# Expert retrieval on one core: v as the stationary operand, both coefficient parts as one moving operand, and 24 tokens instead of 16 handled apart, on the v side too

## The chip, the core and the metric

The kernel runs on one core of a Trainium2 chip. The metric is the device time of one execution in microseconds (us). The core's TensorE (PE) multiplies matrices: it loads a stationary operand of up to 128 columns and streams a moving operand past it. VectorE (DVE), ScalarE (ACT) and GpSimd (POOL) do the rest. SyncE (SP), ACT and POOL issue DMA transfers. Each engine works through its own list of instructions in order and waits where an operand is not ready.

## The reference, cut to what matters

One layer of a decoder for 256 tokens of width 1024: a token mixer, then a feed-forward part made of 16384 experts (128 x 128 product keys), of which each token uses 128 (8 heads x 16). The change is in the second part:

```python
q = (hf @ wq).reshape(T, PEER_HEADS, 2, PEER_QDIM // 2)
s = jnp.einsum('thpd,hpnd->thpn', q, subkeys)
s1, i1 = lax.top_k(s[:, :, 0], 16); s2, i2 = lax.top_k(s[:, :, 1], 16)
top_s, pos = lax.top_k(s1[..., :, None] + s2[..., None, :], 16)     # idx: i1*128 + i2 at pos
w = jax.nn.softmax(top_s, axis=-1)
act = jax.nn.gelu(jnp.einsum('cd,chkd->chk', x_c, u[idx_c]))
coef = w_c * act
out = jnp.einsum('chk,chkd->cd', coef, v[idx_c])                    # u, v: 16384 x 1024
```

The result is added to x, and a last RMSNorm with the gain g_last gives the output.

## The kernel before, in words

Everything but the expert part (the mixer, the projection to the queries, the scores) runs until about 275 us and is not touched. After that the kernel does not gather experts for most tokens. It computes all 128 blocks of 128 experts densely, and multiplies by coefficients that are zero nearly everywhere.

**u stage** (`u_pair`, 64 pairs of blocks). Each block of u (128 experts x 1024) is streamed in by SP as a 512 KB tile `raw`, split by ACT into a rounded part `whi` (L192) and by DVE into the rest `wlo` (L196). `block_t` (L364) then makes 24 matmuls for it: 8 chunks of the width, times three products (whi with the tokens' rounded part `ah`, whi with their rest `al`, wlo with `ah`). The moving operand holds the dense tokens, TD = 240 columns. ACT applies Gelu, and the result stays on the chip in `G`, for all 128 blocks. The tiles `raw`, `whi` and `wlo` have three buffers each, and `slot` loads two to three blocks ahead and splits two ahead.

**The hot part of the u stage** (pairs 32 to 63, 64 slots from about 455 us). Beside the blocks, the coefficients of 8 tokens at a time (30 groups) are scattered: DVE writes one-hot rows (`hot_keys`, `hot_high`), ACT scales (`hot_low`), PE multiplies them (`hot_sum`, 16 matmuls, L1293) into a PSUM tile `pw`, and ACT and DVE multiply it into `G` (`hot_copy`, `hot_use`, L1308). The table `at_slot` says in which slot each of these stands: `hot_sum(k)` in slot 2k+2, `hot_use(k)` in slot 2k+3.

**The 16 tokens left out** (NG = 16, two groups of TG = 8). Their 128 experts each are gathered: POOL fetches 128 rows of u by an indirect DMA (`rows_in`, L1083), and DVE multiplies them with the tokens' rows and sums (`dot`, L1089). Their coefficients then go through DMAs and a transpose back into one-hot form (`few_keys`, `few_sum`, 24 matmuls each, L1326, `few_use`) and into `G`, so that for v they are dense columns like the others (256 in all). For the room, the residual `x2` is written out to DRAM and read back.

**v stage** (128 blocks from 662 us). ACT rounds a row of G to `ch` (L1377), DVE takes the rest `cl` (L1378). The stationary operand is 128 tokens of ch or cl, the moving one half of a row block of v (512 columns of whi or wlo): 12 matmuls of 512 columns for each block (`v_part`, L1389), into four PSUM tiles `acc` of 128 tokens x 512. The residual was put there first by 16 transposes (L1411). ch and cl have two buffers each: those of block k+1 are made when block k-1 is done. The last two blocks are done PSUM tile by PSUM tile, so that the closing norm of a tile can begin while PE works on the next.

## Time and profile before

| what | value |
|---|---|
| median of 3 runs | 1021.89 us (1021.51 to 1022.21) |
| the profiled execution's own time | 1019.87 us |
| its span, first to last instruction | 1018.1 us |
| PE busy | 1003.4 us (99%) |
| DVE busy | 761.1 us (75%) |
| ACT busy | 597.3 us (59%) |
| moved by DMA | 192.87 MB, 189 GB/s over the span |

The span is shorter than the execution's own time by 1.8 us, which lie ahead of the first instruction and behind the last. PE's busy time counts matmuls whose ends are modelled, so 99% says that PE nearly always had a matmul in flight, not that each is as short as it can be. What one matmul costs in a stream is read from start to start: the time of a piece of the chain divided by the number of matmuls in it.

### The profile page before, as it was taken

What the parts mean: (1) busy time and instruction counts of PE and PEld (TensorE: products, weight loads), DVE (VectorE), ACT (ScalarE), POOL (GpSimd) and SP (SyncE); (2) the same over time, 40 slices, a digit from 0 to 9 for tenths busy, and PEclk for the clock granted to TensorE, in tenths of its full rate; (3) what the DMA queues carried; (4) which work ended last, traced back from release to release, by engine and by line L of the source; (5) the groups of instructions that cost most, each with busy time, mean ns of one, the idle gap of its engine ahead of it and who ended that gap; (6) DMA issues with size and microseconds to landing.
All of it is one profiled execution on the core that took longest, in us unless ns stands there. A gap on an engine that the chain in (4) does not pass through costs nothing.

```text
span 1018.1 us, 18964 instructions
## 1 busy us (share of the span) xinstructions
PE 1003.4 (99%) x7394; PEld 926.0 (91%) x7394; DVE 761.1 (75%) x1423; ACT 597.3 (59%) x1090; POOL 53.8 (5%) x69
## 2 busy tenths in 40 slices
PE   9999999999999999999999999999999999999997
PEld 7898999999999999999999999988888888888885
DVE  5888676877889987868999999756666666666664
ACT  7554445665555655648888777545455455454454
POOL 3000010000010001120111100000000000000000
PEclk9999999999999999999999999999999999999999
DMA  8733444566486657675566545545555555555562
GB/s 275 244 103 105 125 113 140 166 199 189 155 286 210 210 192 249 217 279 183 209 209 208 185 153 187 181 166 189 201 189 192 200 186 195 198 189 195 195 211 101
DMA packets 54938, 192.87 MB, mean 189 GB/s; under 512 B 6512, under 2 KB 7968, under 8 KB 54816
## 3 DMA queue, kind: packets, MB, share of 16 engines
q1 hardware_dynamic: 48816, 175.27, 52.2%
q0 software_dynamic: 4448, 14.74, 4.3%
q10 hardware_dynamic: 1584, 1.64, 0.5%
q8 instruction: 58, 0.95, 0.4%
q14 instruction: 32, 0.26, 0.1%
HBM read 188.40 MB, written 3.23 MB: 188 GB/s over the span
## 4 chain that ended last, share of the span: by engine, by line
PE 93%; DVE 4%; ACT 2%; DMA 1%; issue 0%; DVEq 0%; ACTq 0%
PE pj L364 47%; PE acc L1389 34%; PE pw L1293 3%; DVE wlo L196 1%; DMA raw<-in_u_t 1%; PE pS L655 1%; ACT whi L192 1%; PE pT L627 1%; PE pS L496 1%; PE pS L1170 1%; PE pO L286 1%; PE pO L638 0%; PE pO L639 0%; PE pj L760 0%; PE pj L757 0%
## 5 line engine op out<-in xcount | busy, mean ns | idle before, releaser
L196 DVE TENSOR_TENSOR wlo<-raw,whi 128x1024 fp32r<-128x1024 f32 (+2 forms) x329 | 398.9, 1213 | 126.3 <-ACT whi L192 125.3
L192 ACT ACTIVATE whi<-raw 128x1024 fp32r<-128x1024 f32 (+2 forms) x329 | 343.2, 1045 | 125.9 <-PE pj L364 51.2
L364 PE MATMUL pj<-ah,whi 128*128 128x240 f32 (+1 forms) x1344 | 321.3, 282 | 0.3 <-ACT whi L192 0.3
L364 PE MATMUL pj<-al,whi 128*128 128x240 f32 (+1 forms) x1344 | 314.9, 277 | 0.0
L364 PEld LDWEIGHTS pj<-al,whi 128*128 128x128 f32 x1344 | 255.0, 190 | 1.2 <-issue 1.0
L364 PEld LDWEIGHTS pj<-ah,whi 128*128 128x128 f32 x1344 | 254.1, 189 | 2.0 <-issue 1.2
L364 PE MATMUL pj<-ah,wlo 128*128 128x240 f32 (+1 forms) x1344 | 181.1, 277 | 0.0
L364 PEld LDWEIGHTS pj<-ah,wlo 128*128 128x128 f32 x1344 | 166.0, 189 | 0.0
L1389 PE MATMUL acc<-whi,ch 128*128 128x512 f32 x512 | 158.6, 390 | 0.0
L1389 PE MATMUL acc<-wlo,ch 128*128 128x512 f32 x512 | 158.5, 389 | 0.0
L1389 PE MATMUL acc<-whi,cl 128*128 128x512 f32 x512 | 158.5, 390 | 0.0
L1377 ACT ACTIVATE ch<-G 128x256 fp32r<-128x256 f32 x128 | 53.4, 418 | 171.3 <-PE acc L1389 171.3
L1389 PEld LDWEIGHTS acc<-whi,cl 128*128 128x128 f32 x512 | 96.1, 188 | 20.2 <-DVE cl L1378 0.3
L1389 PEld LDWEIGHTS acc<-whi,ch 128*128 128x128 f32 x512 | 96.0, 188 | 20.2 <-ACT ch L1377 0.3
L1389 PEld LDWEIGHTS acc<-wlo,ch 128*128 128x128 f32 x512 | 96.1, 188 | 19.9
L1378 DVE TENSOR_TENSOR cl<-G,ch 128x256 fp32r<-128x256 f32 x128 | 54.4, 426 | 69.5 <-ACT ch L1377 69.5
L1281 ACT ACTIVATE onehot<-onehot,wl 128x128 f16<-128x128 f16 x240 | 76.4, 392 | 18.3 <-DVE onehot L1285 17.6
L364 PE MATMUL pj<-bh,whi 128*128 128x256 f32 x192 | 48.0, 286 | 0.0
L364 PE MATMUL pj<-bl,whi 128*128 128x256 f32 x192 | 47.4, 284 | 0.0
L1293 PE MATMUL pw<-onehot 128*128 128x128 f16 x480 | 33.3, 220 | 4.1 <-DVE G L1308 2.5
L622 ACT ACTIVATE prob<-pS,nm 128x128 f32<-128x128 f32 (+1 forms) x48 | 19.7, 416 | 29.1 <-DVE nm L619 29.1
L1274 DVE TENSOR_TENSOR onehot<-io,keys 128x2048 f16<-128x2048 f16 x30 | 36.6, 1220 | 0.0
(316 smaller groups left out, 902.3 us busy)
## 6 DMA issues: line engine op xcount, KB each, us to landing
raw<-in_u_t SPq DMA_DIRECT2D x128, 512.0 KB, 3.3
raw<-in_v_n SPq DMA_DIRECT2D x128, 512.0 KB, 3.3
raw<-in_w_m SPq DMA_DIRECT2D x16, 512.0 KB, 3.6
raw<-in_w_q SPq DMA_DIRECT2D x16, 512.0 KB, 3.7
raw<-in_w_t SPq DMA_DIRECT2D x15, 512.0 KB, 4.6
raw<-in_w_b SPq DMA_DIRECT2D x8, 512.0 KB, 3.6
raw<-in_w_o SPq DMA_DIRECT2D x8, 512.0 KB, 3.5
sg<-in_w SPq DMA_DIRECT2D x4, 512.0 KB, 6.7
```

The lines of the kernel that those rows point to most:

```text
L192: return [lambda s=slice(u, min(v, n)): nc.scalar.activation(hi[:, s], raws[k][:, s], AF.Copy) for u, v in cuts]
L196: nc.vector.tensor_tensor(lo[:, cs], raws[k][:, cs], hi[:, cs].bitcast(F32), OP.subtract)
L286: nc.tensor.matmul(wb, warm[:, :P], warm, start=True, stop=True)
L364: nc.tensor.matmul(out, (wl if v == 2 else wh)[:, c], (l if v == 1 else h)[:, c], start=(i == 0), stop=(i == len(seq) - 1))
L496: nc.tensor.matmul(hp[:30, :P], flat(wins[j][:, lp // 8, lp % 8]), w1[:, j, lp], start=(lp == 0), stop=(lp == 15))
L622: nc.scalar.activation(p[:, o], src[b], AF.Exp, bias=nm[:, b:b + 1], accum_out=sums[:, b, h:h + 1])
L1274: nc.vector.tensor_tensor(pairs(E[:, 0:2].rearrange("p s t i -> p (s t) i")), numbers(2 * TG), v[:, :, None, :].to_broadcast([P, 2 * TG, 6 ...
L1281: nc.scalar.activation(E[:, 1, t], E[:, 1, t], AF.Copy, scale=wl[:, n:n + 1])
L1293: nc.tensor.matmul(pw[:, t * P:(t + 1) * P], E[:, 0, t], E[:, 2 - s, t], start=(s == 0), stop=(s == 1))
L1377: nc.scalar.activation(ch, g, AF.Copy)
L1378: nc.vector.tensor_tensor(cl, g, ch.bitcast(F32), OP.subtract)
L1389: nc.tensor.matmul(acc[2 * b + d], (cl if q == 1 else ch)[:, tb], (vl if q == 2 else vh)[:, cs], start=False, stop=last and q == 2, skip_g ...
```

## The change

It does four things.

1. NG goes from 16 to 24: three groups of 8 tokens are left out of the dense part, and TD is 232 instead of 240. There are 29 instead of 30 hot groups.
2. The tokens left out stay out on the v side. Their rows of v are gathered as well (24 more indirect DMAs), and DVE adds them up, weighted, in 24 steps `row_sum` in the v stage, one in every third slot. A group of 8 tokens lies on 128 partitions as 16 parts of 8 tokens. Each group's sums go to DRAM (`ys`, 512 KB), come back with 16 parts side by side (`fold_in`, in runs of 64 numbers), and are added up by DVE (`fold`, a reduction over 1024 numbers in each partition). Their norm and output come from `few_add` to `few_out`. The one-hot path of these tokens (`few_keys`, `few_sum`, `few_use`, `dots_end`, `coefs_in`) and the residual's way through DRAM are gone.
3. In the v stage a block of v is stationary, 128 of its columns at a time, and one tile `co` holds ch and cl side by side (2 x 232 columns) as the moving operand: 8 matmuls of 464 columns with whi and 8 of 232 with wlo. The sums lie transposed, 8 PSUM tiles of 128 of the width x 464. The residual is added by DVE at the end (`finish`), and 16 transposes bring the tokens back into rows (`turn_rows`) ahead of the norm.
4. In the hot part `hot_sum(k)` stands in slot 2k+4 instead of 2k+2, and `dot` in every sixth instead of every fourth slot.

```diff
-NG = 16
+NG = 24
+TB = TD // 2
...
     for k in range(ND):
-        at_slot(2 * k + 2, "pre", hot_sum, k)
-        at_slot(2 * k + 3, "first", hot_copy, k)
-        at_slot(2 * k + 3, "pre", hot_use, k)
...
+        at_slot(2 * k + 4, "pre", hot_sum, k)
+        at_slot(2 * k + 5, "first", hot_copy, k)
+        at_slot(2 * k + 5, "pre", hot_use, k)
...
-        for q in (0, 1, 2):
-            for d in ds:
-                cs = slice(d * 512, d * 512 + 512)
-                nc.tensor.matmul(acc[2 * b + d], (cl if q == 1 else ch)[:, tb], (vl if q == 2 else vh)[:, cs],
-                                 start=False, stop=last and q == 2, skip_group_check=True)
+    def v_high(k, w, c):
+        nc.tensor.matmul(acc[c][:, :2 * TD], w[0][:, c * P:(c + 1) * P], coefs[k], start=(k == 0), stop=False,
+                         skip_group_check=True)
+
+    def v_low(k, w, c):
+        nc.tensor.matmul(acc[c][:, small], w[1][:, c * P:(c + 1) * P], coefs[k][:, :TD], start=False,
+                         stop=(k == P - 1), skip_group_check=True)
...
+    def row_sum(n):
+        q, j = divmod(n, TG)
+        t = rows_of_step(NG + n)
+        w = acts[:, q, j:j + 1]
+        if j == 0:
+            sums_of[0] = oh.tile([P, D], F32, name="ysum", bufs=1)
+            nc.vector.tensor_scalar(sums_of[0], t, w, None, OP.mult)
+        else:
+            nc.vector.scalar_tensor_tensor(sums_of[0], t, w, sums_of[0], OP.mult, OP.add)
+        rows_in(NG + n + 2)
+        if j == TG - 1:
+            nc.gpsimd.dma_start(ys[q], sums_of[0])
+
+    def fold_in(q):
+        nc.gpsimd.dma_start(xq[1].rearrange("p (g d) -> p g d", g=16),
+                            ys[q].rearrange("(g t) (c d) -> (t c) g d", t=TG, c=16))
+
+    def fold(q):
+        r = oh.tile([P, 64], F32, name="fold")
+        nc.vector.tensor_reduce(r, xq[1].rearrange("p (g d) -> p d g", g=16), AX.X, OP.add)
+        nc.gpsimd.dma_start(yd[q * TG:(q + 1) * TG].rearrange("t (c d) -> (t c) d", c=16), r)
...
+    for n in range(NG):
+        at_slot(26 + 3 * n, "v", row_sum, n)
+    for q in range(NQ):
+        n = 26 + 3 * (TG * q + TG - 1)
+        at_slot(n + 2, "v", fold_in, q)
+        at_slot(n + 6, "v", fold, q)
...
+    def finish(c):
+        for k in (P - 2, P - 1):
+            v_high(k, ends[k], c)
+            v_low(k, ends[k], c)
+        xc = x2c(c)[:, NG:]
+        nc.vector.tensor_tensor(xc, xc, acc[c][:, small], OP.add)
+        lasts[c] = oh.tile([P, TD], F32, name="last", bufs=3)
+        nc.vector.tensor_tensor(lasts[c], acc[c][:, :TD], xc, OP.add)
```

Where the v stage begins, PE's list read as follows before (pj is the last u block, acc the sums over v):

```order
L364 MATMUL pj<-ah,whi 128x240
L364 MATMUL pj<-al,whi 128x240
L364 MATMUL pj<-ah,wlo 128x240 x8
L1411 MATMUL acc<-ident,x_0_132 128x128 x8
L1411 MATMUL acc<-ident,x_1_133 128x128 x8
L1389 MATMUL acc<-whi,ch 128x512 x2
L1389 MATMUL acc<-whi,cl 128x512 x2
```

and reads now:

```order
L365 MATMUL pj<-ah,whi 128x232
L365 MATMUL pj<-al,whi 128x232
L365 MATMUL pj<-ah,wlo 128x232 x8
L1329 MATMUL acc<-co,whi 128x464 x8
L1333 MATMUL acc<-co,wlo 128x232 x8
```

The transposes between the stages are gone, and the first matmul of a block needs all of co, where it needed ch alone.

In the v stage around slot 53, DVE's list read as follows before (cl and wlo by turns, with buffer numbers):

```order
L1378 TENSOR_TENSOR cl_10169<-G0_2779,ch_10168 128x256
L196 TENSOR_TENSOR wlo_10173<-raw_10144,whi_10172 128x1024
L1378 TENSOR_TENSOR cl_10191<-G0_2779,ch_10190 128x256
L196 TENSOR_TENSOR wlo_10195<-raw_10166,whi_10194 128x1024
L1378 TENSOR_TENSOR cl_10213<-G0_2779,ch_10212 128x256
L196 TENSOR_TENSOR wlo_10217<-raw_10188,whi_10216 128x1024
```

and reads now (ysum is the running row sum, fold the reduction of what fold_in brought into xq):

```order
L1364 TENSOR_SCALAR ysum_10184<-row0_5871,acts_2790 128x1024
L1326 TENSOR_TENSOR co_10205<-G0_2779,co_10205 128x232
L197 TENSOR_TENSOR wlo_10209<-raw_10175,whi_10208 128x1024
L1326 TENSOR_TENSOR co_10230<-G0_2779,co_10230 128x232
L197 TENSOR_TENSOR wlo_10234<-raw_10203,whi_10233 128x1024
L1326 TENSOR_TENSOR co_10255<-G0_2779,co_10255 128x232
L197 TENSOR_TENSOR wlo_10259<-raw_10228,whi_10258 128x1024
L1366 SCALAR_TENSOR_TENSOR ysum_10184<-row1_5872,acts_2790,ysum_10184 128x1024
L1377 TENSOR_REDUCE fold_10264<-xq_5873 128x64
L1326 TENSOR_TENSOR co_10285<-G0_2779,co_10285 128x232
```

A row sum stands behind every third wlo, and in this slot the fold too, ahead of the next block's co.

On POOL the last rows before were these (x is the residual coming back from DRAM):

```order
L1083 DMA x_0_132<-in_u_n,sidx 128x1024 x8
L1097 DMA ads<-x_1_133 128x8
L1112 DMA x_1_133<-ads 8x16x8 x2
L1073 DMA x_0_132<-x2s_2792 128x512 x2
L1073 DMA x_1_133<-x2s_2793 128x512 x2
L1462 TENSOR_SCALAR raw<-raw,lr 128x512
```

and around the first fold they are these now:

```order
L1080 DMA row_5872<-in_v_n,sidx 128x1024
L1369 DMA ys_2798<-ysum 128x1024
L1372 DMA xq<-ys_2798 128x16x64
L1080 DMA row_5871<-in_v_n,sidx 128x1024
L1080 DMA row_5872<-in_v_n,sidx 128x1024
L1378 DMA yd<-fold 128x64
```

POOL, which issued nothing in the v stage, now has the gathers of v there, the way of the row sums through DRAM (ys out, xq back) between them.

## Rows read from the trace of the kernel before

**Rows 1.** The page's busy times and PE's granted clock in 40 slices.
```profile
PE 1003.4 (99%) x7394; PEld 926.0 (91%) x7394; DVE 761.1 (75%) x1423; ACT 597.3 (59%) x1090; POOL 53.8 (5%) x69
PEclk9999999999999999999999999999999999999999
```

**Rows 2.** The page's chain of waits: shares of the span by line.
```profile
PE pj L364 47%; PE acc L1389 34%; PE pw L1293 3%; DVE wlo L196 1%; DMA raw<-in_u_t 1%; PE pS L655 1%; ACT whi L192 1%; PE pT L627 1%; PE pS L496 1%; PE pS L1170 1%; PE pO L286 1%; PE pO L638 0%; PE pO L639 0%; PE pj L760 0%; PE pj L757 0%
```

**Rows 3.** Windows: length, busy of PE, PEld, DVE, ACT, POOL; clock, DMA share, GB/s.
```profile
278.00:455.00 177.00, 176.72 (x1578) 176.53 (x1577) 155.23 (x458) 98.85 (x123) 19.80 (x23) 1.00 0.68 231
463.00:606.00 143.00, 143.00 (x1447) 142.14 (x1447) 133.43 (x185) 119.83 (x297) 13.69 (x10) 1.00 0.57 192
661.92:1005.23 343.31, 343.31 (x1517) 284.29 (x1516) 208.10 (x253) 172.06 (x252) 0.00 (x0) 1.00 0.57 190
```

**Rows 4.** Pieces of the chain in order of time: start, us, what, count.
```profile
219.98 7.68 PE pj L364 x64
...
231.64 0.89 PE pS L1170 x8
...
428.42 21.52 PE pj L364 x192
...
496.43 0.91 PE pw L1293 x16
...
602.15 1.41 PE pw L1326 x24
...
617.98 1.35 PE pw L1326 x24
```

**Rows 5.** PE's timeline at the first hot sum: start, us, what, [idle before].
```profile
455.56 0.23 PE L1293 MATMUL pw<-onehot 128*128 128x128 f16 x1 [0.26 <-DVE onehot L1285]
...
458.10 1.09 PE L1293 MATMUL pw<-onehot 128*128 128x128 f16 x7 [0.96 <-ACT onehot L1281]
```

**Rows 6.** Waits from 463 to 660 us: us, times, longest.
```profile
PE pw L1293 <- DVE G L1308: 2.5, 2, 1.5
```

**Rows 7.** Timeline at the entry to the v stage.
```profile
660.26 1.91 PE L1411 MATMUL acc<-ident,x 128*128 128x128 f32 x16
...
661.64 0.75 DVE L1378 TENSOR_TENSOR cl<-G,ch 128x256 fp32r<-128x256 f32 x2
661.92 0.71 PE L1389 MATMUL acc<-whi,ch 128*128 128x512 f32 x2
```

**Rows 8.** Groups of instructions: busy, mean ns of one, idle before and releasers.
```profile
L196 DVE TENSOR_TENSOR wlo<-raw,whi 128x1024 fp32r<-128x1024 f32 (+2 forms) x329 | 398.9, 1213 | 126.3 <-ACT whi L192 125.3 <-PE pO L354 0.3
L192 ACT ACTIVATE whi<-raw 128x1024 fp32r<-128x1024 f32 (+2 forms) x329 | 343.2, 1045 | 125.9 <-PE pj L364 51.2 <-DMA raw<-in_u_t 34.7 <-issue 10.7
L1378 DVE TENSOR_TENSOR cl<-G,ch 128x256 fp32r<-128x256 f32 x128 | 54.4, 426 | 69.5 <-ACT ch L1377 69.5
L1377 ACT ACTIVATE ch<-G 128x256 fp32r<-128x256 f32 x128 | 53.4, 418 | 171.3 <-PE acc L1389 171.3
L1089 DVE SCALAR_TENSOR_TENSOR x<-x,x 128x1024 f32<-128x1024 f32 x10 | 12.2, 1217 | 0.0
```

**Rows 9.** DMA issues: queue, count, KB each, median us to landing.
```profile
raw<-in_v_n SPq DMA_DIRECT2D x128, 512.0 KB, 3.3
xhs<-xhd POOLq DMA_DIRECT2D x2, 512.0 KB, 6.2
x2s<-x POOLq DMA_DIRECT2D x4, 256.0 KB, 8.8
x<-xhs POOLq DMA_DIRECT2D x2, 512.0 KB, 4.8
...
kcb<-kraw POOLq DMA_DIRECT2D x2, 128.0 KB, 5.4
```

**Rows 10.** Timeline of the kernel's end.
```profile
1010.88 0.60 ACT L1433 ACTIVATE squares<-acc 128x512 f32<-128x512 f32 x1 [0.49 <-PE acc L1389]
...
1012.57 0.88 DVE L1471 SCALAR_TENSOR_TENSOR raw<-acc,lr,x 128x256 f32<-128x256 f32 x2
```

More of the change, by code (lines that the diff above doesn't have):

```diff
@@ L1243, in body @@
             pre = (lambda: tokens_out((e - 4) // 2),), ()
[L1244 to L1246 removed]
+        if e == 16:
             pre = (lambda: tokens_in(0),), ()
[L1248 removed]
+        if 22 <= e < 25:
             pre = (lambda: rows_in(e - 22),), ()
@@ L1258, in body @@
     ps = PB.enter_context(tc.tile_pool(name="pb", bufs=2, space=PSUM, reuse_waits="tile"))
-    G[1] = top.enter_context(tc.tile_pool(name="gb", bufs=1, reuse_waits="tile")).tile([P, 64, T], F32, name="G1")
+    G[1] = top.enter_context(tc.tile_pool(name="gb", bufs=1, reuse_waits="tile")).tile([P, 64, TD], F32, name="G1")
+    wide_rows = top.enter_context(tc.tile_pool(name="rows", bufs=1, reuse_waits="tile"))
+    rows_wide += [wide_rows.tile([P, D], F32, name=f"row{k}") for k in range(2)]
+    xq.append(wide_rows.tile([P, D], F32, name="xq"))
     OH = ExitStack()
@@ L1309, in hot_use @@
         spots["tokens"] += TG
-    few = [flat(t).bitcast(BF).rearrange("p (k t i) -> p k t i", k=2, i=P) for t in x2]
-    def few_keys(q):
-        for s in range(2):
-            nc.vector.tensor_tensor(pairs(few[0][:, s]), numbers(TG),
-                                    keys[:, q, s, :, None, :].to_broadcast([P, TG, 64, 2]), OP.is_equal)
-        for k in range(3):
-            v = cs[:, k, q * TG:(q + 1) * TG, None, :].to_broadcast([P, TG, 64, 2])
-            nc.vector.tensor_tensor(pairs(few[1][:, k] if k < 2 else few[0][:, 1]), pairs(few[0][:, 1]), v, OP.mult)
-    def few_sum(q):
-        pw = wide()
-        for t in range(TG):
-            for k, v in enumerate((few[1][:, 0, t], few[1][:, 1, t], few[0][:, 1, t])):
-                nc.tensor.matmul(pw[:, t * P:(t + 1) * P], few[0][:, 0, t], v, start=(k == 0), stop=(k == 2))
-        hot["few", q] = pw
-    def few_use(q):
-        pv = hot.pop(("few", q)).rearrange("p (t i) -> p i t", t=TG)
-        for k in range(2):
-            nc.scalar.activation(G[k][:, :, q * TG:(q + 1) * TG], pv[:, 64 * k:64 * k + 64], AF.Copy)
     ND = TD // TG
@@ L1406, in v_use, with weights_in, weights_mix @@
-        return f
-    for c in range(NC):
-        for b in range(2):
-            o = acc[2 * b + c // 4][:, (c % 4) * P:(c % 4 + 1) * P]
-            nc.tensor.matmul(o, x2c(c)[:, b * P:(b + 1) * P], ident, start=(c % 4 == 0), stop=False,
-                             is_transpose=True, skip_group_check=True)
+        return f
+    sums_of = [None]
+    def weights_in():
+        nc.scalar.activation(acts, acts, AF.Gelu)
+    def weights_mix():
+        nc.vector.tensor_tensor(acts, acts, mix, OP.mult)
@@ new lines, in few_add, with few_square, few_factor, few_out @@
+    def few_add():
+        nc.vector.tensor_tensor(few[0], few[0], few[1], OP.add)
+    def few_square():
+        nc.scalar.activation(few[1], few[0], AF.Square, scale=1.0 / 32.0, accum_out=fs[:, 0:1])
+    def few_factor():
+        v, r, t, w = (fs[:, k:k + 1] for k in range(1, 5))
+        nc.vector.tensor_scalar(v, fs[:, 0:1], EPS, None, OP.add)
+        nc.scalar.activation(r, v, AF.Sqrt)
+    def few_out():
+        v, r, t, w = (fs[:, k:k + 1] for k in range(1, 5))
+        nc.vector.reciprocal(r, r)
+        nc.vector.tensor_tensor(t, r, r, OP.mult)
+        nc.vector.tensor_tensor(t, t, v, OP.mult)
+        nc.vector.tensor_scalar(t, t, -0.5, 1.5, OP.mult, OP.add)
+        nc.vector.tensor_tensor(w, r, t, OP.mult)
+        nc.vector.scalar_tensor_tensor(few[0], few[0], w, gf[:NG], OP.mult, OP.mult)
+        nc.sync.dma_start(a["out"][0:NG], few[0])
@@ new lines, in body @@
+    for n in range(2 * TG, NG):
+        at_slot(1 + 3 * (n - 2 * TG), "v", dot, n)
+    at_slot(23, "v", weights_in)
+    at_slot(24, "v", weights_mix)
+    for n in range(NG):
+        at_slot(26 + 3 * n, "v", row_sum, n)
+    for q in range(NQ):
+        n = 26 + 3 * (TG * q + TG - 1)
+        at_slot(n + 2, "v", fold_in, q)
+        at_slot(n + 6, "v", fold, q)
+    at_slot(n + 8, "v", few_in)
+    at_slot(n + 12, "v", few_add)
+    at_slot(n + 13, "v", lambda: table(AF.Sqrt))
+    at_slot(n + 13, "v", few_square)
```

239 lines of the change are left out of this document (105 added, 134 removed).

## The prediction

> **What bounds the kernel now.** I read the page's busy times first, then the chain of waits, then windows by stage. PE is busy for 1003.4 of 1018.1 us, at a granted clock of nine tenths or more of the upper level, 2.4 GHz, in all 40 slices [rows 1]. The chain agrees: the block matmuls of the u stage and the projections (L364) hold 47% of the span, those of the v stage (L1389) 34%, and no other engine more than a few per cent [rows 2]. By windows, PE has no idle time in the v stage (343.31 of 343.31 us) nor in most of the hot part, while DVE is busy for 208.10 of 343.31 us in the former and 133.43 of 143.00 us in the latter [rows 3]. So the time is a count of matmuls times the pace of each, plus the few places where PE waits; DVE is the engine that could become the bound.
>
> The pace is read from pieces of the chain in which PE runs without a break [rows 4]: 7.68 us for 64 matmuls of 256 columns is 120.0 ns each, 21.52 us for 192 of 240 columns is 112.1 ns. In the v stage, 343.31 us for 1517 matmuls of 512 columns is 226.3 ns [rows 3]. From 256 to 512 columns a column costs (226.3 - 120.0) / 256 = 0.415 ns. But 8 matmuls of only 128 columns in float32 took 0.89 us, 111.2 ns each [rows 4], against 0.91 us for 16 in 16 bits. So below 240 columns there is a floor for 4-byte operands close to what 240 columns cost.
>
> **The change part by part.** Durations are those of the profiled execution, whose own time is 1019.87 us; the median of the runs shown lies 2.0 us above it, and I carry the difference over to that median.
>
> *Matmuls of the u stage, 240 to 232 columns.* 128 x 24 = 3072 matmuls. If nothing but the floor counts, they stay at 112.1 ns and nothing is saved. If the step from 256 to 240 columns goes on ((120.0 - 112.1) / 16 = 0.49 ns a column), they take 108.2 ns and 12.1 us go. The row nearest in operand type and stationary size is the floor's 111.2 ns, but it has plain float32 operands in short series; I take 110, a little below it: 3072 x 2.1 ns = -6.5 us.
>
> *Matmuls of the v stage.* Before, a block takes 12 x 226.3 = 2716 ns. Now it has 8 of 464 columns, 226.3 - 48 x 0.415 = 206.4 ns each, and 8 of 232 at 110: 2531 ns. That is -0.185 us for each of 126 blocks (the last two are in the tail below), -23.3 us. With 112.1 or 108.2 ns for the small ones it is -21.2 or -25.1. The stationary operands go from 12 to 16 in a block; they cost only through this floor, since in the u stage 24 such loads a block lie beside matmuls half as wide.
>
> The Trainium skill weighs in on this floor: "TensorE: Matmul & The Clock Gate", section "LDWEIGHTS (loading the stationary operand)", gives a load as its columns divided by 1.2 GHz, 106.7 ns for 128, and its section "Back-to-back issue gap" gives a warm matmul as its columns at 2.4 GHz plus 2.5 ns, 102.5 ns for 240. By the greater of the two a u matmul would take 106.7 ns with 240 columns as with 232, so that the u stage would save nothing, and a v block 8 x 195.8 + 8 x 106.7 = 2420 ns instead of 12 x 215.8 = 2590, -21.4 us. The trace's 112.1 and 226.3 ns lie above both figures, so I keep to rows for the size; the direction is a rival below.
>
> *One-hot sums.* One hot group fewer is -0.9 us, the two `few_sum` are 1.41 + 1.35, -2.8 us [rows 4]. Together -3.7.
>
> *Stalls in the hot part.* The first hot sum began at 455.56 and ended at 459.19 us, since ACT and DVE were late with its one-hot rows [rows 5]; it should take 0.9, so with the 0.26 ahead of it 2.9 us were lost. It now stands two slots later, some 5.3 us, which covers that: -2.9. Twice PE waited for DVE to free `pw`, for 2.5 us [rows 6]; both waits stand behind a `few_sum`, which took one of the two buffers, and go: -2.5. What is late next there is DVE: 133.43 of 143.00 us with a dot every fourth slot is 5.94 us in a pair of 6.37; a dot (1.22 us [rows 8]) every sixth slot instead of every fourth takes 0.2 us off a pair, and a pair of PE becomes 48 x 2.1 ns shorter, 6.27. That is 0.92 full on average, more towards the end; I put no stall there. Together -5.4.
>
> *Entry to the v stage.* The 16 transposes took from 660.26 to 661.92 us, and beside them ACT and DVE made the first ch and cl. Gone, they leave PE idle for the same time: the first matmul now needs cl too, which began at 661.64 and takes 0.43 [rows 7, 8], so that it starts at about 662.1. +0.2.
>
> *Row sums and folds.* Let a slot of the v stage be 2.53 us, and T the start of slot 47, in which the first group's last row sum stands. In a slot, ACT makes ch (0.42) and whi (1.05) once PE has left the block before; then DVE has made cl at about 1.1 and wlo at 2.9, and a row sum behind it (1.22, by the dot's row) at 4.15 [rows 8]. The next cl is due at 5.06, so a row sum alone stops nobody, and on average DVE has 2 x 1.65 + 2.85 = 6.15 us of work in three slots, 7.6 us. The fold is another matter. Row sum ends at T + 4.15, `ys` goes out (512 KB), POOL waits for it, then `fold_in` brings 512 KB back in 2048 runs of 256 bytes; the fold stands in slot 53, behind a row sum, and so begins at T + 15.2 + 4.15 at the earliest. Even on time it ends at T + 20.6 (a reduction of 1024 numbers at the row sum's 1.2), and cl behind it is 0.75 us late for PE. In the trace such a write took 6.2 us (`xhs`; 8.8 for the four `x2s`) and a read of the same size 4.8 in 4 KB runs [rows 9]. No row shows one with 2048 runs. From below it takes the 4.8; from above, if runs are what costs, 16 times the 5.4 us that `kcb` took for 128 runs of 1 KB, 86 us. I take twice the nearest row, 10: the way is then 16.2 us, 1.0 over the 15.2 that it has, and the first two folds stop PE for 1.75 each. The third has no row sum ahead of it; by the same count it has 14.4 us and stops PE for 1.8. Together +5.3; from below 1.5.
>
> On such runs the Trainium skill says, in "DMA: Bandwidth & Descriptors", section "Why small descriptors are slow (HBM only)", that 256-byte ones lose 27% to a fixed cost for each. By that `fold_in` would take an estimated 4.8 x 1.27 = 6.1 us and the folds stop PE for 1.5 in all, the end from below; no run here shows it yet.
>
> The gathers of v themselves (24 x 512 KB, one in 7.6 us) add 69 GB/s to 512 KB in 2.53 us, 207. The v stage moved 190 GB/s at a share of 0.57 [rows 3], so 276 would be 0.83. A block's 3.3 us to landing [rows 9] has 5.06 us, two slots, from the freeing of its buffer. I count nothing; if the cover is gone, this is late by what landing exceeds 5.
>
> *Tail.* Before, the last two blocks begin at 1005.23 and the span ends at 1018.1 [rows 3], 12.9 us. Now each of the 8 chunks has 2 x (206.4 + 110) = 633 ns of matmuls, two adds of DVE (0.43 each by cl's row), and two transposes (0.22 by the floor): about 0.85 a chunk on either engine, the last transposes done at 7.9 instead of 5.4. Then ACT has two sums of squares to do (0.60 each [rows 10], and a read-out) where one was left, and the two factors come one after the other. Against the old end, where the last squares began at 1010.88 and the last product at 1012.57 [rows 10], I make that +4.9 in all.
>
> Sum: -6.5 - 23.3 - 3.7 - 5.4 + 0.2 + 5.3 + 4.9 = -28.5, so 991.4 for a profiled execution and 1021.89 - 28.5 = **993.4 us** as a median.
>
> **The rivals.**
>
> *Folds hidden, no floor.* The path through DRAM lands in time (1.5 instead of 5.3), and the small matmuls go on falling to 108.2 ns (u -12.1, v -25.1): 993.4 - 3.8 - 5.6 - 1.8 = 982; with one of the two, 984 to 990. For it: 256 to 240 columns did bring 7.9 ns. Against it: the 111.2 ns of 128 columns.
>
> *The floor holds at 112.1.* Loads of 128 columns already set the pace at 240, so u saves nothing (+6.5) and v 2.1 less: 1002. For it: 111.2 and 112.1 are nearly the same. This is what the skill's rule on loads, weighed above, would make of it.
>
> *DVE becomes the bound.* Late in the hot part `hot_use` covers more blocks and DVE passes PE; at one dot (1.22 us) too much for each of the last four dots that is 4.9: 998. Against it: four slots of lead.
>
> *The folds are late, and the kernel is slower.* DVE stops in order behind each fold, and nothing makes cl meanwhile. The three folds stop PE for 3 x (way - 14.4) or so. All other terms are -33.8, so this decides from 11.3 us a fold: a `fold_in` of over 20 us beside a 6.2 us write. At 26 us it is 3 x 17.8 = 53 and the time 1021.9 - 33.8 + 53 = 1041. For it: 2048 runs have no like in the trace, and the queue shares its engines with v. Against it: 10 us is already twice the nearest row. Between (14 to 20 us) lie 1004 to 1023.
>
> **How the numbers follow.** Forecast 0.52 (its own range 989 to 998), hidden folds or no floor 0.18, floor 0.11, DVE 0.05, folds between 0.08, slower 0.06. The measurement tells 0.2%, 2 us, from no change: the runs before lie within 0.7. Faster 0.93, same 0.01 (out of the late folds), slower 0.06. From 982 to 1006 I leave out most of the late folds and little below, under 2 in 10.
>
> **What would show it.** PE from start to start: near 206 ns for 464 columns, 110 for 232. Windows: about 2.53 us a block in the v stage. The first hot sum at 0.91 us, no wait of `pw` on DVE. In the waits of DVE, the fold on DMA, three times, and PE or its loads on `co` behind it. At the end, some 18 us from the first of the last two blocks. I am wrong if DVE's or ACT's idle time in the v stage vanishes and PE waits there in most slots, or if the block pace is above 2.6 us without such waits.

## The result and the profile after

The changed kernel takes 1012.58 us (median of 4 runs, 1009.96 to 1013.66) against 1021.89 (1021.51 to 1022.21): a ratio of 0.9908, 95% interval 0.9895 to 0.9922. The forecast of 993.4 and its range of 982 to 1006 miss it: 9.3 us were gained where 28.5 were forecast. The profiled run took 1009.96 us. The page's busy times and granted clock, which answer [rows 1]:

```profile
PE 979.0 (97%) x7841; PEld 938.0 (93%) x7841; DVE 791.8 (79%) x1469; ACT 593.0 (59%) x1079; POOL 104.3 (10%) x106
PEclk9999999999999999999999999999999999999996
```

The chain by line, for [rows 2]:

```profile
PE pj L365 50%; PE acc L1329 20%; PE acc L1333 10%; PE pw L1272 3%; PE pS L656 1%; DVE wlo L197 1%; DMA ys<-ysum 1%; PE pT L628 1%; PE pS L497 1%; PE pS L1148 1%; ACT whi L193 1%; DMA xg<-in_x 1%; PE pO L639 0%; PE pO L640 0%; DMA raw<-in_v_n 0%
```

PE is still the bound, but a DMA (`ys<-ysum`) stands in the chain, and in the last slice PE rests and its granted clock falls. Windows put the lost time in its place (start and end, length, busy of PE, PEld, DVE, ACT, POOL, clock, DMA share, GB/s): the u stage from its first narrow matmul to its last, the first 126 blocks of v, and the last two blocks with all that follows. Before:

```profile
275.53:660.42 384.89, 380.55 (x3620) 377.76 (x3618) 340.07 (x716) 263.81 (x525) 35.70 (x37) 1.00 0.61 208
661.92:1004.78 342.86, 342.86 (x1516) 283.91 (x1514) 208.00 (x253) 171.81 (x251) 0.00 (x0) 1.00 0.57 190
1004.78:1018.09 13.31, 6.00 (x25) 4.24 (x23) 4.86 (x17) 6.36 (x15) 1.57 (x1) 0.83 0.21 79
```

and after:

```profile
274.62:647.29 372.67, 372.67 (x3553) 371.70 (x3550) 330.12 (x695) 260.07 (x510) 33.70 (x34) 1.00 0.63 215
649.02:981.72 332.70, 327.09 (x2017) 302.49 (x2017) 242.38 (x304) 172.56 (x257) 53.80 (x41) 1.00 0.74 254
981.72:1008.19 26.47, 7.82 (x50) 6.37 (x48) 10.94 (x32) 5.07 (x13) 0.00 (x0) 0.71 0.11 36
```

| stretch | forecast | measured | missed by |
|---|---|---|---|
| ahead of the u stage | 0 | -0.9 | -0.9 |
| u stage with hot part (-6.5 - 3.7 - 5.4) | -15.6 | -12.2 | +3.4 |
| entry to v | +0.2 | +0.2 | 0 |
| 126 blocks (-23.3 + 5.3) | -18.0 | -10.2 | +7.8 |
| tail | +4.9 | +13.2 | +8.3 |
| sum | -28.5 | -9.9 | +18.6 |

The 0.9 us ahead of the u stage are scatter: in seven other profiles of this document it begins at 274.4 to 276.6 us.

In the u stage an unbroken piece of the chain (start, us, what, count) now reads as below, for [rows 4]: 32.16 us for 288 matmuls is 111.7 ns each, not 110. The first one-hot sum takes 0.91 us, as forecast.

```profile
426.50 32.16 PE pj L365 x288
458.66 0.91 PE pw L1272 x16
```

In the v stage a block without a stop is 8 high matmuls in 1.69 us and 8 low ones in 0.89 (chain from 797 us on): 211 and 111 ns, 2.58 us a block instead of 2.53. So the low ones came as forecast and the high ones are 5 ns dearer.

```profile
797.49 1.69 PE acc L1329 x8
799.18 0.89 PE acc L1333 x8
```

The rest of the 7.8 us is stops. Below are the waits of PE from the second block to the 126th (us, times, longest) and the chain ahead of the longest. With the slower matmuls right behind them the stops cost 7.1 us (332.70 less 126 x 2.584), where 5.3 were forecast.

```profile
PE acc L1329 <- DVE co L1326: 5.6, 4, 2.1
```

```profile
773.31 1.21 DVE ysum L1366
...
774.78 1.98 POOL row L1080
776.75 7.75 DMA ys<-ysum
...
784.60 0.10 DVE ysum L1364
...
785.27 0.41 DVE co L1326
...
785.72 1.96 PE acc L1329 x8
```

The four stops are of 2.13, 0.91, 0.92 and 1.65 us. The first group's last row sum ends at 774.5; POOL issues the next gather ahead of `ys`, `ys` takes 7.75 us, and the second group's first row sum, which overwrites the single `ysum`, holds DVE until it has landed. Behind it stands `co`, for which PE waits. I had looked for waits at the folds' data. They landed in time, in 6.5 us (DMA issues of the v stage, for [rows 9]), and the first two folds, each behind a row sum, stop PE for 0.9 us each by their own length, 1.98 us instead of 1.2; the third, without a row sum ahead of it, stops nobody:

```profile
raw<-in_v_n SPq DMA_DIRECT2D x123, 512.0 KB, 4.2
ys<-ysum POOLq DMA_DIRECT2D x3, 512.0 KB, 6.1
xq<-ys POOLq DMA_DIRECT2D x3, 512.0 KB, 6.5
```

```profile
L1377 DVE TENSOR_REDUCE fold<-xq 128x64 f32<-128x1024 f32 x3 | 5.9, 1981 | 0.0
```

A third kind of stop comes at 955.78, and SP's timeline shows its cause (start, us, queue, line, count): the 24 rows' output, L1408, waited on SP's queue for DVE until 948.36, and the weight loads behind it waited too; the chain then reads `DMA raw<-in_v_n` for 4.22 us, ACT, DVE, PE.

```profile
935.88 5.56 SPq L182 DMA_DIRECT2D raw<-in_v_n  x3
948.36 0.40 SPq L1408 DMA_DIRECT2D out_n<-row  x1
948.85 6.92 SPq L182 DMA_DIRECT2D raw<-in_v_n  x4
```

At the end, the last product (for [rows 10]) starts at 995.44, 13.7 us into the tail where it was 7.8 before: 5.9 more, of the 4.9 forecast, a first wait of 0.6 among them. But from there to the end it is 12.8 us instead of 5.5. The DMA view from 993 to the end, in 40 slices:

```profile
DMA  0000222313122312222222222222222222110000
GB/s 0 0 0 0 65 49 59 65 27 59 59 49 75 59 65 81 81 81 81 75 97 92 75 97 108 102 97 92 102 102 97 102 108 81 75 38 5 0 0 0
```

A share of two to three tenths and some 100 GB/s: the four output transfers of 116 rows keep about a quarter of the engines busy. Before, five transfers of 128 rows (three of 512 columns, two of 256) landed in 2.4 to 3.0 us.

### The profile page after: what moved, and what is told of

Same layout as the page of the kernel before. It is cut to its first block, busy times and chain, and to the rows that moved or that the text cites. A ratio compares the mean times of both kernels' runs of the same rounds, so it can differ in the third digit from the quotient of the medians.

```text
span 1008.2 us, 19956 instructions
## 1 busy us (share of the span) xinstructions
PE 979.0 (97%) x7841; PEld 938.0 (93%) x7841; DVE 791.8 (79%) x1469; ACT 593.0 (59%) x1079; POOL 104.3 (10%) x106
## 4 chain that ended last, share of the span: by engine, by line
PE 91%; DVE 4%; DMA 2%; ACT 1%; issue 1%; POOL 0%; SPq 0%; ACTq 0%; DVEq 0%
PE pj L365 50%; PE acc L1329 20%; PE acc L1333 10%; PE pw L1272 3%; PE pS L656 1%; DVE wlo L197 1%; DMA ys<-ysum 1%; PE pT L628 1%; PE pS L497 1%; PE pS L1148 1%; ACT whi L193 1%; DMA xg<-in_x 1%; PE pO L639 0%; PE pO L640 0%; DMA raw<-in_v_n 0%
## 5 line engine op out<-in xcount | busy, mean ns | idle before, releaser
L365 PE MATMUL pj<-ah,whi 128*128 128x232 f32 (+1 forms) x1344 | 319.2, 280 | 0.0
L365 PE MATMUL pj<-al,whi 128*128 128x232 f32 (+1 forms) x1344 | 313.2, 276 | 0.1
L1329 PE MATMUL acc<-co,whi 128*128 128x464 f32 x1024 | 240.8, 375 | 7.9 <-DVE co L1326 7.9
L1329 PEld LDWEIGHTS acc<-co,whi 128*128 128x128 f32 x1024 | 183.2, 189 | 26.9 <-DVE co L1326 7.4
L365 PE MATMUL pj<-ah,wlo 128*128 128x232 f32 (+1 forms) x1344 | 179.9, 276 | 0.0
L1333 PEld LDWEIGHTS acc<-co,wlo 128*128 128x128 f32 x1024 | 135.0, 190 | 6.3
L1333 PE MATMUL acc<-co,wlo 128*128 128x232 f32 x1024 | 136.9, 274 | 0.0
L1325 ACT ACTIVATE co<-G 128x232 fp32r<-128x232 f32 x128 | 50.7, 397 | 144.3 <-PE acc L1333 144.3
L1326 DVE TENSOR_TENSOR co<-G,co 128x232 fp32r<-128x232 f32 x128 | 50.9, 398 | 33.2 <-ACT co L1325 33.2
L365 PEld LDWEIGHTS pj<-bl,whi 128*128 128x128 f32 x192 | 36.3, 189 | 0.0
```

Source lines behind the costliest of these rows:

```text
L365: nc.tensor.matmul(out, (wl if v == 2 else wh)[:, c], (l if v == 1 else h)[:, c], start=(i == 0), stop=(i == len(seq) - 1))
L1325: nc.scalar.activation(t[:, :TD], g, AF.Copy)
L1326: nc.vector.tensor_tensor(t[:, small], g, t[:, :TD].bitcast(F32), OP.subtract)
L1329: nc.tensor.matmul(acc[c][:, :2 * TD], w[0][:, c * P:(c + 1) * P], coefs[k], start=(k == 0), stop=False, skip_group_check=True)
L1333: nc.tensor.matmul(acc[c][:, small], w[1][:, c * P:(c + 1) * P], coefs[k][:, :TD], start=False, stop=(k == P - 1), skip_group_check=True)
```

## The experiments

Each states its theories' expectations as they stood before it ran; where no other kernel is named, the edit is to the changed one. The diffs are shortened to the lines that carry the edit.

### Output of 116 rows cut into 112 and 4

```diff
-        nc.scalar.dma_start(rows_of(b)[:, halves_of[0]], yo[b][:, halves_of[0]])
+        for r in CUTS:  # slice(0, 112), slice(112, 116)
+            nc.scalar.dma_start(rows_of(b)[r, halves_of[0]], yo[b][r, halves_of[0]])
```

> The changed kernel with each of its four output transfers of 116 rows cut into one of 112 rows and one of 4. Theory (a transfer is shared out over as many DMA engines as divide its rows, and 116 = 4 x 29 leaves 4 of 16): the end, 12 us from the first issue to the last byte before, needs about 4 to 5 us, 7 to 8 us less; median 1004 to 1006 against 1012.6. Rival (the transfers wait behind other traffic or on their queues): no more than 1 us less, and the two more transfers add up to 1 us. Second rival (their lines of 2 KB are slow whatever the rows): no change either.

### Rows at the end as 128 and 104

```diff
-    turned[...][:TB, ...], lasts[c][:, b * TB:(b + 1) * TB]
+    turned[...][:TBS[b], ...], lasts[c][:, CUT[b]]   # 0:128, 128:232; sent as 128, and 96 + 8
```

> The changed kernel with the 232 rows at the end cut into blocks of 128 and 104 rows instead of twice 116, the second sent as 96 and 8 rows. By the theory of the engines (128 and 96 rows over 16, 8 rows over 8) the same gain as the cut in 112 and 4 within 1 us, 1004 to 1006: the small transfer is off the last place's way. By the rivals (other traffic, queue, line length) no change, 1011 to 1014.

The first took 1008.96 us (1003.09 to 1012.01; ratio to the kernel before 0.9854, 0.9817 to 0.9892), the second 1007.12 (1002.83 to 1011.31; 0.9869, 0.9836 to 0.9903). The medians fell by 3.6 and 5.5 us, less than the 7 to 8 forecast, and the runs scatter by 9 us, so the tail itself decides. Second kernel, tail in the windows and DMA view from 994 to the end:

```profile
982.69:1001.06 18.37, 7.83 (x50) 6.37 (x48) 10.93 (x32) 5.07 (x13) 0.00 (x0) 0.81 0.15 52
```

```profile
DMA  0000000002999999900002999999751000000000
```

The tail is 18.37 us instead of 26.47, 8.1 less (in the first kernel, from 991.05 us on, 19.19, 7.3 less), and the engines run at nine tenths, where they ran at two to three. That is the theory; the rivals of queue and line length fall, since queues and lines of 2 KB are the same. The Trainium skill has the rule, in "DMA: Bandwidth & Descriptors", section "Why a DMA increments its semaphore by 16 and not by 1": a transfer goes to the largest number of engines up to 16 that divides its slowest dimension, which for 116 is 4. The share of two to three tenths agrees. Had I weighed it, the 116 rows would have been a rival with some 8 us.

In the first kernel's profile PE waits 10.8 us in the v stage behind its entry, and behind two of its stops, of 3.29 and 2.20 us, the granted clock fell. Windows of the stop and of the block behind it:

```profile
846.00:853.46 7.46, 4.17 (x29) 3.71 (x27) 2.34 (x4) 3.03 (x5) 0.93 (x1) 1.00 0.77 279
853.46:857.58 4.12, 4.12 (x16) 3.77 (x16) 2.52 (x3) 0.15 (x1) 1.64 (x2) 0.59 0.58 198
```

At 0.59 of 2.4 GHz, that is mostly at the lower level of 1.2, the block of 16 matmuls takes 4.12 us for 2.58. So a stop costs more than its length, now and then. This goes some way to explain the scatter: the second kernel's four runs, of 1002.83, 1005.36, 1008.87 and 1011.31 us, had mean granted clocks of 0.995, 0.994, 0.993 and 0.990. The first kernel's do not fall into such an order.

### The waits of the v stage

On top of 128 and 104 rows:

```diff
-            sums_of[0] = oh.tile([P, D], F32, name="ysum", bufs=1)
+            sums_of[0] = oh.tile([P, D], F32, name="ysum", bufs=2)
-        rows_in(NG + n + 2)
         if j == TG - 1:
             nc.gpsimd.dma_start(ys[q], sums_of[0])
+        rows_in(NG + n + 2)
-        at_slot(n + 6, "v", fold, q)
+        at_slot(n + 7, "v", fold, q, 0)   # half the columns each
+        at_slot(n + 8, "v", fold, q, 1)
-        nc.sync.dma_start(a["out"][0:NG], few[0])
+        nc.gpsimd.dma_start(a["out"][0:NG], few[0])
```

> The kernel with 128 and 104 rows at the end, and four edits against the waits of its v stage: two buffers for the row sums, their DMA issued ahead of the next gather, each fold made in two halves two slots apart and one to two slots later, and the 24 rows' output sent on GpSimd's queue instead of SP's. Theory (TensorE's stops at 785, 794, 857 and 955 us of the changed kernel come of these four, and the spread of its runs too, since a stop can cost the clock behind it): the idle time there goes from 0.8 to 2.3 us each to under 0.2, about 5 us less than with the rows alone (1007.1), 1000 to 1003, and a spread under 3 us. Rival (the stops come of late weight loads in a DMA that is 0.75 to 0.84 busy, whatever waits where): they show up elsewhere, 1005 to 1009 with the same spread of 8 to 9 us.

It took 998.90 us (997.81 to 1000.79), ratio 0.978, 0.9762 to 0.9797: 8.2 us less than with the rows alone, and a spread of 3.0 instead of 8.5. The waits of PE in the v stage, and its windows (126 blocks, tail):

```profile
PE acc L1329 <- DVE co L1326: 0.6, 1, 0.6
```

```profile
650.95:978.36 327.41, 326.65 (x2016) 302.21 (x2017) 242.18 (x307) 173.10 (x257) 59.32 (x42) 1.00 0.73 258
978.36:996.80 18.44, 7.82 (x50) 6.36 (x48) 10.94 (x32) 5.07 (x13) 0.00 (x0) 0.84 0.15 52
```

The stops at 785 and 955 us are gone, the second fold's too; 0.6 us stays at the first. There the rival is right: ahead of that stop the chain has `DMA raw<-in_v_n` for 6.90 us, a weight load at the time when the fold's data come in. The four edits were made at once, so which of them took which stop is argued from the chains, not shown by runs of their own; the chains of the stops near 785 and 955 us have the same causes in the profiles of the two kernels above. The profiles with and without the waits differ by 6.1 us in the 126 blocks (333.47 and 327.41), the medians by 8.2.

### The new one-hot table on the kernel before

```diff
-        at_slot(2 * k + 2, "pre", hot_sum, k)
+        at_slot(2 * k + 4, "pre", hot_sum, k)   # its operands in slots 2k to 2k+2
```

> The kernel before with the new table of the one-hot work alone (each sum two slots later, its operands made one to two slots earlier before it). The prediction's step: the first one-hot sum no longer waits for its operands, 2.9 us less, and the two waits for the wide PSUM tile (2.5 us) go only if they come of the table and not of the sums for the 16 tokens. Expected 1019 (2.9 gone) or 1016.5 (both gone). Rival (the wait is taken over by another one in the hot part): 1021 to 1022, no change.

1018.22 us (1017.41 to 1019.97, 9 runs), ratio 0.9968, 0.9954 to 0.9982: 3.1 us, where the interval runs from 1.8 to 4.7. In its profile the first sum still waits for 0.4 us, and the u stage is 2.5 us shorter (382.37 for 384.89). The wait for `pw` is still there (waits of PE, 463 to 660 us), so it belongs to the sums for the 16 tokens, as I had it:

```profile
PE pw L1293 <- DVE G L1308: 2.4, 2, 1.4
```

### Matmuls by width

```diff
+                hi = lambda c: nc.tensor.matmul(acc[c][:, :m], w[0][:, c * P:(c + 1) * P], flat_ah[:, at:at + m], ...)
+                lo = lambda c: nc.tensor.matmul(acc[c][:, to:to + n], w[1][:, c * P:(c + 1) * P], flat_ah[:, at:at + n], ...)
```

> Measures matmuls by width: in the v stage six blocks each with (hi, lo) columns from 512 + 256 down to 400 + 200 on constant moving data in order of all hi then all lo, three of them with a shifted source, a shifted target or hi and lo in turn; in the first half of the u stage 232, 240, 248 and 256 columns by groups of four pairs. It leaves out what the coefficients carry into the sums, so its time is no time of the kernel. The prediction's line through 256 and 512 columns (120.0 and 226.7 ns) gives 206.7 at 464, 213 at 480, 200 at 448, 180 at 400. Theory (464 columns are dear whatever is in them): about 212 at 464 here too, and the widths around tell whether it is a step or a bend. Rival 1 (the data, written by ScalarE and VectorE just before): 206 to 207 here. Rival 2 (the order, eight high ones and then eight low ones): 207 only where hi and lo take turns. Rival 3 (where the data or sums lie, 464 x 4 bytes after a buffer's start): only the shifted groups show 212. For the u stage: floor theory 112 at 232 and 240, 116 to 120 above; no floor 109 to 110 at 232.

Windows over four pairs of u blocks each, 192 matmuls and a few others, at 232, 240, 248 and 256 columns:

```profile
364.60:386.37 21.77, 21.77 (x198) 1.00 0.63 206
386.37:408.02 21.65, 21.65 (x194) 1.00 0.73 258
408.02:430.35 22.33, 22.33 (x197) 1.00 0.60 201
430.35:453.15 22.80, 22.80 (x195) 1.00 0.80 276
```

From 256 to 240 columns 6 ns go, from 240 to 232 none: the floor. Six v blocks of 464 + 232 columns and of 512 + 512:

```profile
766.40:781.92 15.52, 15.52 (x99) 1.00 0.74 271
950.06:972.45 22.39, 22.39 (x98) 1.00 0.58 205
```

2.587 us a block with constant moving data too, so rival 1 falls; rival 3 falls as well (groups with a shifted source or target took 2.59 too). In turn it is 2.561: rival 2 holds in part. The surprise is 512 columns: 233 ns, not the 226.7 of the kernel before.

### Orders, targets, roles

```diff
+                still = lambda c: ah[:, c, 0:P]
+                mm(c % banks, part(h, c), move(0, x))      # 8, 4, 2, 1 targets
+                mm(c, still(c), half(h, c % 2, x))         # weights move
+                mm(2 * b + d, still(q), half(q // 2, d, m)) # order of the kernel before
+                mm(c, still(c), move(0, x))                # constants alone
```

> Measures why a 512-column matmul took 226.7 ns in the kernel before and 233.3 in the widths' measurement (464: 212.5 against 206.4 forecast): six blocks each, 16 (as before: 12) matmuls, some of it changed at a time; the sums are not the kernel's. Theory A (the target: four PSUM tiles in turn before, eight now): 226.7 with four banks or fewer, 233.3 with eight. Theory B (which operand moves: before the loaded weights moved): 226.7 only where the weights move. Theory C (a stationary block is used twice before): 226.7 where each is used twice. Theory D (where the stationary block lies: a piece of 512 bytes out of the 4 KB rows of the weights, against coefficients): 226.7 with constant stationary blocks. None of them: 233.3 in all, and the difference lies in something else than the matmul's operands. For 464 + 232 columns: 323.7 ns a pair in the order of now, 320.4 in turn; a lag or another target tells whether the gain is of the width's change or of the target.

Windows of 96 matmuls each: 512 columns with the weights moving against constant stationary blocks, 512 columns with constants alone, 464 columns with each stationary block used twice:

```profile
738.68:761.08 22.40, 22.40 (x97) 1.00 0.52 176
817.08:838.86 21.78, 21.78 (x97) 1.00 0.81 286
968.81:989.07 20.26, 20.26 (x98) 1.00 0.57 194
```

Theories A to D fell as stated: 233.3 ns at 512 columns whatever the targets, roles or order, down to the kernel before's own order and with constant stationary blocks too, and 226.8 only with constants against constants. 464 columns by themselves take 211.1 ns. For 464 + 232 columns the gain belongs to taking turns as such: 2.560 us with either target, 2.580 where the low products lag by four. That left the operands' places, or who writes them.

### Places

```diff
+                still = (whole_a if "const" in kind else w[h])[:, c % 7 * P + s:c % 7 * P + s + P]   # s, o: 0 or 8 columns
+                mm(still, move(x))                                                                    # al[:, o:o + x]
```

> In the measurement of orders only constant stationary blocks with constant moving data gave the 226.7 ns of the kernel before at 512 columns, the same blocks against the loaded weights 233.3 in either role. Theory E (where the operands lie: the weights' buffers begin at 0 modulo 64 bytes of a partition in the changed kernel and at 32 in the kernel before, the constants and coefficients at 32 in both): groups whose stationary block is moved by 32 bytes, or whose moving data are, change between 226.7 and 233.3; if the two must agree, 0 with 0 and 32 with 32 give 226.7 and the mixed ones 233.3; if 32 is needed of both, only 32 with 32. With the weights as stationary blocks moved by 32 bytes against constants at 32: 226.7. Theory F (buffers that a DMA or an engine writes meanwhile are dear to read): constant blocks 226.7 and weights 233.3 whatever the shift. For 464 + 232 columns a block takes 2.567 us where 512 takes 226.7, and 2.586 where it takes 233.3.

Windows of 96 matmuls of 512 columns each, first four with constants: neither shifted, the moving one, the stationary one, both; then weights against constants: neither shifted, stationary, both, moving.

```profile
649.41:671.20 21.79, 21.79 (x98) 1.00 0.74 249
671.20:693.60 22.40, 22.40 (x97) 1.00 0.85 288
693.60:716.00 22.40, 22.40 (x98) 1.00 0.84 289
716.00:737.79 21.79, 21.79 (x98) 1.00 0.85 287
...
799.59:821.98 22.39, 22.39 (x99) 1.00 0.42 137
821.98:844.38 22.40, 22.40 (x98) 1.00 0.57 187
844.38:866.77 22.39, 22.39 (x97) 1.00 0.59 192
866.77:888.53 21.76, 21.76 (x97) 1.00 0.57 191
```

21.8 us is 227 ns each, 22.4 is 233. As the program places them, the constants begin at 96 modulo 128 bytes of a partition and the weights at 0, and a shift adds 32. All eight groups follow one rule: 227 where the two operands begin at the same place modulo 128, 233 where the places differ by 32 or 64. Two more groups, with 16 bytes of shift, took 233 as well. The weights shifted by 32 against constants at 96 (22.40) show that modulo 64, which I had expected, is not enough. Modulo 128 itself is not told from a larger power of two: in the fast groups, as in the kernel before, the places agree modulo 512 too. Theory F falls: the last group reads weights at 227. Two narrower groups, constants at equal places, 480 and 448 columns:

```profile
995.26:1016.08 20.82, 20.82 (x98) 1.00 0.64 209
1016.08:1035.91 19.83, 19.83 (x98) 1.00 0.56 181
```

216.9 and 206.6 ns: from 512 down to 448 a column is worth 0.31 ns, not the 0.415 between 512 and 256 on which my 206.4 for 464 columns rests. At 0.31 it is 211.6, and the trace has 211; but in the trace the two operands begin at different places. At equal places a block of 464 + 232 columns took 2.566 us here (737.79 to 753.18 us, six blocks), and 2.58 to 2.59 where the places differ.

### A pad of 32 bytes in the kernel before

```diff
+    oh.tile([P, 8], F32, name="pad", bufs=1)
```

> The kernel before with a pad of 32 bytes ahead of its coefficients' buffers, nothing else: they then begin at 0 modulo 128 bytes of a partition, where the weights' begin at 96; before both begin at 96. Theory E2 (a 512-column matmul takes 226.7 ns where its two operands begin at the same place modulo 128 bytes, else 233.3; the measurement of places agrees in all its groups at 512 columns): 1536 matmuls at 6.6 ns more, the v stage 10 us longer, 1031 to 1033. Rival (the constant data of that measurement are what matters): no change, 1020 to 1023.

1032.98 us (1028.48 to 1035.50), ratio 1.0113, 1.0093 to 1.0133: slower, with not one instruction changed. Its 126 blocks against the 342.86 us above:

```profile
660.48:1013.37 352.89, 352.89 (x1515) 284.16 (x1514) 207.97 (x253) 171.67 (x251) 0.00 (x0) 1.00 0.53 185
```

10.0 us for 1512 matmuls, 6.6 ns each, as the theory has it for places 32 bytes apart.

### High and low in turn, pads, equal places, folds in quarters

All on the kernel without the waits, except the two named as alone.

```diff
                 for c in range(NC):
                     v_high(k, w, c)
-                for c in range(NC):
                     v_low(k, w, c)
```

> The same with each column group's high and low product in turn instead of eight high ones and then eight low ones. In the measurement of widths 464 + 232 columns in turn took 2.563 us a block against 2.586, so 126 blocks give 2.9 us: 997 to 1000. Rival (the low product now needs the low half of the weights 0.2 us after the block's start instead of 1.7 us, and VectorE makes it late): a wait in many blocks, slower than the kernel before this edit by 2 us or more.

```diff
+    const.tile([P, 8], F32, name="pad")
+    oh.tile([P, 8], F32, name="pad", bufs=1)
```

> The kernel with rows, waits and turns, and two pads of 32 bytes, after which the weights' buffers begin at 32 modulo 64 bytes of a partition, as in the kernel before, and the coefficients' stay at 32. By theory E (the operands' places) a block of the v stage loses up to 19 ns, 2.4 us in all: 993.5 to 995.5 against 996.65. By theory F no change, 996 to 998. The u stage's matmuls (whose moving operand then begins at 0 and its weights at 32) may change by some 0.5 ns each, 1.5 us either way.

> The changed kernel with the two pads alone. By theory E the v block goes from 2.582 us to about 2.56, by theory F it stays 2.58; the time, which carries the spread of the changed kernel's waits, 1008 to 1013.

```diff
+    oh.tile([P, 24], F32, name="pad", bufs=1)
-        t = coefs[k] = oh.tile([P, 2 * TD], F32R, name="co")
+        t = coefs[k] = oh.tile([P, 2 * TD + 16], F32R, name="co")[:, :2 * TD]
```

> The changed kernel with its coefficients' buffers at the weights' place modulo 128 bytes (both at 0; a pad of 96 bytes, and 1920 instead of 1856 bytes each). By theory E2 a v block takes 2.567 us instead of 2.584, as constants on matched places did, 2.1 us in all; the rest of the 55 ns by which a block missed the forecast stays. The time carries the waits' spread: 1008 to 1014. Rival: 2.584 as now.

> The kernel with rows, waits and turns, and matched places. By theory E2 a block goes from 2.585 us (in turn, unmatched) to 2.560, 3.1 us in all: 993 to 995 against 996.65. Rival: no change.

```diff
-        hs = slice(32 * h, 32 * h + 32)
+        hs = slice(16 * h, 16 * h + 16)   # in slots n + 7 to n + 10
```

> The same with each fold in four parts in four slots instead of two in two. TensorE's last stops behind the folds (0.6 to 1.9 us in the profiles so far) should fall under 0.2 us each: 1 to 1.5 us less, 992 to 994, which would be the fastest of all. Rival (a stop behind a fold comes from the fold's data being late and not from VectorE's load): no change.

| kernel | us, median and range | ratio, 95% interval | v block, us: even, odd |
|---|---|---|---|
| changed | 1012.58, 1009.96 to 1013.66 | 0.9908, 0.9895 to 0.9922 | 2.583, 2.584 |
| pads alone | 1013.81, 1010.29 to 1022.74 | 0.9932, 0.9902 to 0.9962 | 2.576, 2.597 |
| equal places alone | 1014.09, 1010.61 to 1017.28 | 0.9914, 0.9888 to 0.994 | 2.581, 2.566 |
| rows and waits | 998.90, 997.81 to 1000.79 | 0.978, 0.9762 to 0.9797 | 2.583, 2.584 |
| + turns | 996.65, 995.70 to 998.72 | 0.9754, 0.9735 to 0.9773 | 2.568, 2.586 |
| + turns, pads | 998.45, 996.99 to 999.48 | 0.9774, 0.9746 to 0.9803 | 2.559, 2.581 |
| + turns, equal places | 995.99, 994.86 to 996.96 | 0.9742, 0.9725 to 0.9759 | 2.567, 2.559 |
| + folds in quarters | 996.21, 995.17 to 998.83 | 0.9742, 0.9725 to 0.9759 | 2.567, 2.559 |

(The last row is on top of the one above it. A block's time is the median from start to start, of the even and of the odd blocks among the 126 apart: they use the two buffers of `co` by turns, which begin at different places.) In turn every second block is faster, 2.568 against 2.586, some 0.8 us over the 126; the median fell by 2.2 us, which the overlap of the intervals leaves open. The many waits of the rival did not come: 1.5 us in two stops. The pads were put by the rule modulo 64. By the rule modulo 128 they make the places equal in the odd blocks (coefficients and weights both at 32), and just these are the slow ones, 2.581 against 2.559. With "equal places" the two buffers begin at 128 and at 0 modulo 256, the weights at 0. The odd blocks, equal modulo 256 too, took what was expected, 2.566 in the old order and 2.559 in turn; the even ones, 128 bytes apart, 2.581 and 2.567. So at these widths modulo 128 is not the rule, and what it is stays open. No time stands apart from the one without. Quarters of folds changed nothing: of the three stops of 0.6 to 0.8 us that are left, those at 804.61 and 857.68 have a late weight load ahead of them,

```profile
794.42 6.99 DMA raw<-in_v_n
...
801.43 1.07 ACT whi L193
...
802.52 0.32 DVE wlo L197
```

(the last kernel's chain to its stop at 804.61). So the rival's outcome came, but not for its reason: DVE waited for no fold's data. The last four kernels are hardly told apart; all are faster than both the kernel before, by 2.3 to 2.6%, and the changed one, by 1.4 to 1.6% of its median.

## Why the prediction was wrong, step by step

*Tail, +4.9: the largest miss, 8.3 us.* The compute was sized about right, 5.9 us for 4.9, though the last two blocks before began at 1004.78, not at 1005.23 as I had read. That the same bytes in 116 rows go out as in 128 was assumed without being said. Two cuts of the rows took back 7.3 and 8.1 us. Failed step: the end taken over from [rows 10] with its output transfers as they were.

*v matmuls, -23.3.* A block measured 2.584 us for 2.531; 126 x 53 ns is 6.7 us. The failed number is 206.4 ns for 464 columns, a straight line through 256 and 512; measured alone they take 211.1. Some 18 of the 53 ns go with the operands' places (blocks at equal places took 2.566 us); the other 35 are the line's, since near 512 a column is worth 0.31 ns. The small ones were right: 111 for 110. My 226.3 ns were also a little low: the 1517 counts matmuls that only touch the window, and 342.86 us for 126 x 12 is 226.8, so that a block before took 2.720 us, not 2.716.

*u matmuls, -6.5.* The floor held, the rival to which I gave 0.11: 240 and 232 columns measured 112.8 and 113.4 ns with what stood between them. If sums and stalls gave the 9.1 us forecast, 3.1 are left for the u matmuls; the unbroken pieces alone give 1.3. This is the direction that the rule on loads had in the Trainium skill ("TensorE: Matmul & The Clock Gate", section "LDWEIGHTS (loading the stationary operand)"), and I took 110 all the same, below every row that I had. The 102.5 ns that I quoted beside it from the Trainium skill (same page, section "Back-to-back issue gap") is there the gap of a single matmul, not the pace of a stream.

*Sums and hot-part stalls, -3.7 and -5.4: as forecast in place and cause.* No idle time of PE is left there, so DVE did not become the bound either. The first sum's wait, moved alone, brought 3.1 us for 2.9, and the two waits for `pw` left only with the sums behind which they stood.

*Row sums and folds, +5.3.* The stops cost 7.1 us. That this is near is luck, since the mechanism was wrong: nobody waited for `fold_in`, which came in 6.5 us, not 10. What stopped PE was the single `ysum`, which I had not followed past its write (2.13 us), the fold's own 1.98 us for 1.2 (0.9 twice), and an output on SP's queue (1.65). The first and the last are of the kind that a count of the buffers and of the queue behind each waiting instruction finds; I counted POOL's and left SP's out. The Trainium skill ("DMA: Bandwidth & Descriptors", section "Why small descriptors are slow (HBM only)") counts 11 cycles for 8 of data at 256 bytes. Its 27% is a share of the 11, so that the estimate by it is 4.8 x 11 / 8 = 6.6 us, not my 6.1, and the trace's 6.5 agrees.

*The gathers of v, counted at nothing.* The DMA share was 0.74 on average and 0.84 at its highest (800 to 850 us), where I had worked out 0.83, and raw landed in 4.2 us instead of 3.3. That was mostly hidden, but late loads of about 7 us make the last stops, and one of 7.45 us the longest of all, 3.29 us in the kernel with 112 and 4 rows.

*The slower rival (late folds)* did not happen; `fold_in` in 6.5 us is far from its 20.

## What to carry to other kernels

Before a transfer's shape changes, look at how many rows it has: 116 instead of 128 left a quarter of the engines here, and it cost 8 us because nothing at the kernel's end hides it. Where a change adds instructions on several engines, write down for each buffer who must have let it go and for each queue what stands behind the one that waits: here a few such waits of 0.8 to 2.3 us cost 6 us in the profiles and 8 between the medians, since some of them also cost the clock. And do not draw a line between two widths of a matmul that lie a factor of two apart; measure the width itself.
